# Macaron decoder step: the first two weight chunks multiplied half by half, idle products on TensorE ahead of them, and a pinned order at the start

## The chip, the cores and the metric

The kernel runs on one core of a Trainium2 chip. The metric is the device time of one execution in microseconds (us). TensorE (PE) multiplies, VectorE (DVE), ScalarE (ACT) and GpSimd (POOL) do the elementwise work, and SyncE (SP) issues nearly all DMAs.

## What is computed

Two layers of a decoder trunk, for a prompt of 256 tokens and 8 single-token samples that share all weights. The change touches only what comes first: the input norm and the first SwiGLU block.

```python
def trunk(x, ...):
    for i in range(DEPTH):                      # DEPTH = 2, D_MODEL = 1024, D_FF = 2816
        h = rmsnorm(x, norm_ffn1[i])
        x = x + 0.5 * swiglu(h, w_ffn1_gate[i], w_ffn1_up[i], w_ffn1_down[i])
...
def swiglu(x, w_gate, w_up, w_down):
    return (jax.nn.silu(x @ w_gate) * (x @ w_up)) @ w_down
```

All inputs are float32.

## The kernel before

**Tiling.** The 264 columns (256 prompt tokens, 8 samples) are the moving operand of every projection, with the 1024 features in eight blocks of 128 rows (index k). Weights come in *chunks* of 256 output columns; a chunk has two *halves* of four k blocks, each 128x1024 elements (512 KB). Chunk 0 is gate, chunk 1 is up, and so on in turns. Two output blocks of 128 (index j) make a chunk, each in its own PSUM bank (`pj`).

**Precision.** A product is made of three: the value is split into a rounded part (`xh`, `wh`) and a rest (`xl`, `wl`), and PE adds xh·wh, xl·wh and xh·wl. So each half goes through three steps in class `Weights`: `_load` (L88) issues the DMA to `raw`, `_round` (L98) casts `raw` to `wh`, `_split` (L109) subtracts to get `wl`. There are six `raw` buffers and five each of `wh` and `wl`; a buffer is loaded anew when the step that reads it last is done. `advance` (L125), called from `Flow.tick`, does one split and one round and loads what fits. `W.hi` and `W.lo` say which engine rounds ("s" ACT, "v" DVE) and which splits ("p" POOL, "v" DVE).

**The start.** `start` (L449) loads the samples with the first gains (`small`) and x. PE transposes the samples and gains into `pr` (L474), and the two halves of x, 16 blocks of 128x128, into four PSUM banks `px` (L494). Blocks k and k+4 share a bank. For each k ACT writes `xh` (L322) and DVE `xl` (L324) in `Norm.split`; then DVE copies `px` to `xT` (L503). ACT also sums squares (L485) for the norm; `rsqrt` (L280) and `newton` (L293 to L296) turn them into `rr`, PE spreads `rr` over the partitions (`pb`, L514), and DVE copies that to `R` (L517). The norm factor is applied after the matmul, in `evac`, so the first products need `xh`, `xl` and weights but not `R`.

**The first projection.** `project` with `late_lo` (L360) does chunks 0 and 1 together, 96 matmuls: first all products with `wh` (chunk 0: eight k with xh, eight with xl; then chunk 1), then all with `wl`. Halves are loaded and rounded in the order chunk 0 first half, chunk 0 second half, chunk 1 first half, chunk 1 second half. The first and second are rounded by DVE, the rest by ACT; the first three are split by POOL. From chunk 2 on (L300 to L302), each chunk's three products follow one another for every k.

**Order.** A scheduler places instructions by priority, except those wrapped in `pin` (`tc.keep_in_program_order`), which keep the order in which they are written. Each engine then runs its list strictly in order.

Of the kernel before, what the change touches and what calls it, by code (L numbers as in the profile page):

```python
# [12 lines left out]
ALU = mybir.AluOpType  # L13
# [3 lines left out]
P = 128  # L17
D = 1024
KT = D // P
T = 256  # L20
# [35 lines left out]
class Weights:  # L56
# [31 lines left out]
    def _load(self):  # L88
        i = self.n_load
        parts, n = self.halves[i]  # L90
        raw = self.pool.tile([P, HK, 256], F32, tag="raw", name=f"raw{i}", bufs=RAW_BUFS)
        for src, at in parts:
            dst = raw[:, :n] if len(parts) == 1 else raw.rearrange("p (k s) n -> p k s n", s=2)[:, :, at]
            self.nc.sync.dma_start(dst, src.rearrange("(k p) n -> p k n", p=P))
        self.raw[i] = raw
        self.n_load += 1

    def _round(self):  # L98
# [6 lines left out]
        self.pin(copy(wh[:, :n], self.raw[i][:, :n]))  # L105
        self.ready[i] = wh
        self.n_round += 1

# [108 lines left out]
def trunk_step(ctx: ExitStack, tc: tile.TileContext, ins, consts, outs, stop=None):  # L217
# [69 lines left out]
        act(dst, dst, AF.Exp, scale=-0.5)  # L287

    def newton(dst, src, tmp, scale=1.0, out=None):
        if scale == 1.0:  # L290
            nc.vector.scalar_tensor_tensor(tmp, src, EPS, dst, op0=ALU.add, op1=ALU.mult)
        else:
            nc.vector.tensor_scalar(tmp, src, scale, EPS, op0=ALU.mult, op1=ALU.add)  # L293
            nc.vector.tensor_mul(tmp, tmp, dst)
        nc.vector.scalar_tensor_tensor(tmp, tmp, -0.5, dst, op0=ALU.mult, op1=ALU.mult)
        nc.vector.scalar_tensor_tensor(dst if out is None else out, tmp, 1.5, dst, op0=ALU.add, op1=ALU.mult)  # L296

    def mm3(ps, w, rh, rl, first, last, s=slice(None)):
        wh, wl = w
# [53 lines left out]
    def project(nch, rh, rl, evac, kt_major=2, need=None, before=None, late_lo=False):  # L353
        if not callable(rh):
            rh, rl = (lambda k, t=rh: t[:, k]), (lambda k, t=rl: t[:, k])
        done = 0
        if kt_major:
            ws = [W.get() for _ in range(kt_major)]
            pss = [(c, j, mm_bank(f"pj{c}_{j}")) for c in range(kt_major) for j in range(2)]
            if late_lo:  # L360
                for first in (True, False):
                    for c in range(kt_major):
                        for r in (rh, rl) if first else (rh,):
                            for k in range(KT):
                                w = ws[c](k)[0 if first else 1]
                                for j in range(2):
                                    nc.tensor.matmul(
                                        pss[2 * c + j][2][:, :NC],
                                        w[:, j * P : j * P + P],
                                        r(k),  # L370
                                        start=first and k == 0 and r is rh,
                                        stop=not first and k == KT - 1,
                                    )
                                if k % 4 == 3 and (first or k < KT - 1 or c < kt_major - 1):
                                    flow.tick()
# [37 lines left out]
    def cols(w, c, k0=0, k1=None):  # L413
        return w[k0 : (k1 or w.shape[0]), c * 256 : (c + 1) * 256]

    def add_project(cs, early=False):
        n = 0 if early else 2
        if n:
            W.add(*cs[:n])
        for c in cs[n:]:  # L420
            W.add(c)

    def reg_ffn(name, l):
        cs = [cols(ins[f"w_{name}_{kind}"][l], p) for p in range(FB // 2) for kind in ("gate", "up")]
        add_project(cs, early=name == "ffn1" and l == 0)
# [23 lines left out]
    def start(norm):  # L449
# [13 lines left out]
        nc.vector.memset(ones_d, 1.0 / D)  # L463
        nc.vector.memset(ones_1, 1.0)
        use_set(LNEXP)
        W.preload(4)
        W.pin = pin = tc.keep_in_program_order
        W.lo, W.hi = ("p",), ("v",)
        xn, sm = ring.tiles["x"], ring.tiles["small"]
        with tc.high_priority(offset=1000):  # L470
            ns = NB + 2
            pr = aux_bank("pr")
            for k in range(KT):
                nc.tensor.transpose(pr[:, ns * k : ns * (k + 1)], sm[:ns, k * P : k * P + P], ident[:ns, :ns])  # L474
            prv = pr[:, : ns * KT].rearrange("p (k r) -> p k r", r=ns)
            pin(nc.vector.tensor_copy(gains[:, :, :2], prv[:, :, NB:]))
            xs, gs = prv[:, :, :NB], cp.tile([P, KT, NB], F32, name="gs")
            pin(nc.vector.tensor_copy(xT[:, :, T:], xs))
            pin(nc.vector.tensor_mul(gs, xs, gains[:, :, :1].broadcast_to([P, KT, NB])))
            ss, rr, rt = (cp.tile([P, 3], F32, name=n) for n in ("ss0", "rr0", "rt0"))  # L480
            nc.vector.memset(ss, 1.0)
            junk = memT.rearrange("p k n -> p (k n)")

            def square(i, n, src):
                pin(nc.scalar.activation(junk[:n, :D], src, AF.Square, accum_out=ss[:n, i : i + 1]))  # L485

            square(0, P, xn[:, :D])
            pin(nc.scalar.copy(xh[:, :, T:], gs))
            pin(nc.vector.tensor_sub(xl[:, :, T:], gs, xh[:, :, T:].bitcast(F32)))
            px = [aux_bank("px") if k < 3 else mm_bank("px") for k in range(KT // 2)]  # L490
            px = [b[:, i * T : i * T + T] for i in range(2) for b in px]
            for i in range(2):
                for k in range(KT):
                    nc.tensor.transpose(px[k][:, i * P : i * P + P], xn[:, i * D + k * P : i * D + k * P + P], ident)  # L494
            W.advance()
            for k in range(KT):
                if k == 2:
                    W.advance()
                norm.split(k, px[k], T)
            W.hi = ("s",)  # L500
            W.advance()
            for k in (3, 7, 0, 4, 1, 5, 2, 6):
                pin(nc.vector.tensor_copy(xT[:, k, :T], px[k]))  # L503
            square(1, P, xn[:, D:])
            W.advance()
            square(2, NB, sm[:NB, :D])
            rsqrt(rr, ss, 1.0 / D)
            newton(rr, ss, rt, 1.0 / D)
        W.pin = lambda ins: ins
        W.lo = ("v",)  # L510
        with tc.high_priority(offset=1000):
# [5 lines left out]
            nc.vector.tensor_copy(norm.R, pb[:, :NC])  # L517
        norm.done = True
        use_set(SILU)
        flow.spawn(0, prepare())  # L520

# [978 lines left out]
```

## Time and profile before

| | us |
|---|---|
| median of 3 runs | 1332.32 |
| lowest, highest | 1332.09, 1333.97 |
| the profiled execution, its own time | 1333.74 |
| its span, first to last instruction | 1331.9 |
| PE busy | 1300.5 (98%) |
| DVE, ACT, POOL busy | 842.7, 671.4, 311.2 |

The profiled execution is one run, 1.4 us above the median; times worked out from the trace are compared with its own 1333.74 us. [...]

### The profile page before, as it was taken

The numbers are of one execution on the slowest core, as the hardware profiler recorded it, in microseconds if no ns is written. First come the engines' busy times: TensorE is split into PE (matmuls) and PEld (weight loads), VectorE is DVE, ScalarE is ACT, GpSimd is POOL, SyncE is SP. The second block draws the span as 40 slices with busy tenths as digits, with TensorE's granted clock in tenths as the row PEclk, the third lists the DMA queues.
The fourth block names the chain that finished last, engine by engine and source line by source line (L and its number), as shares of the span: only waits on it lengthen the run. The fifth ranks groups of instructions, "written<-read, shape, count | busy, mean of one in ns | idle before, by whom it ended". The sixth has DMA issues, their size and how long they took to land. (4 is left out here: it accounts for less than half of the span.)

```text
span 1331.9 us, 26153 instructions
## 1 busy us (share of the span) xinstructions
PE 1300.5 (98%) x10420; PEld 1260.0 (95%) x10420; DVE 842.7 (63%) x1586; ACT 671.4 (50%) x1058; POOL 311.2 (23%) x246
## 2 busy tenths in 40 slices
PE   8999999999999999999999999999999997999997
PEld 8999999999879999999999999999998787999996
DVE  6555567769826655465555446968699439766454
ACT  6454444455545555544545545574664445445532
POOL 3211331222641111231111231000015427111220
PEclk9999999999999999999999999999999999999999
DMA  8796565646997666556666566545359994776550
GB/s 278 224 296 186 160 191 182 187 142 220 338 340 230 185 178 186 173 179 188 189 177 182 165 182 187 175 147 174 120 168 300 357 282 127 224 224 204 173 158 34
DMA packets 277435, 266.76 MB, mean 200 GB/s; under 512 B 8697, under 2 KB 275961, under 8 KB 277314
## 3 DMA queue, kind: packets, MB, share of 16 engines
q1 hardware_dynamic: 271486, 259.78, 63.6%
q10 hardware_dynamic: 5828, 5.32, 1.2%
q8 instruction: 82, 1.34, 0.4%
q14 instruction: 39, 0.32, 0.1%
HBM read 255.00 MB, written 10.07 MB: 199 GB/s over the span
## 5 line engine op out<-in xcount | busy, mean ns | idle before, releaser
L117 DVE TENSOR_TENSOR wl<-raw,wh 128x1024 fp32r<-128x1024 f32 (+1 forms) x347 | 431.7, 1249 | 250.3 <-ACT wh L105 235.5
L300 PE MATMUL pj<-xh,wh 128*128 128x264 f32 x1952 | 562.0, 288 | 7.6 <-DVE g L669 5.6
L301 PE MATMUL pj<-xl,wh 128*128 128x264 f32 x1952 | 554.6, 284 | 0.0
L302 PE MATMUL pj<-xh,wl 128*128 128x264 f32 x1952 | 554.0, 284 | 0.0
L105 ACT CAST wh<-raw 128x1024 fp32r<-128x1024 f32 (+1 forms) x406 | 415.0, 1032 | 251.5 <-PE pj L301 132.9
L300 PEld LDWEIGHTS pj<-xh,wh 128*128 128x128 f32 x1952 | 368.8, 189 | 9.9 <-DVE g L669 5.8
L301 PEld LDWEIGHTS pj<-xl,wh 128*128 128x128 f32 x1952 | 369.1, 189 | 0.3
L302 PEld LDWEIGHTS pj<-xh,wl 128*128 128x128 f32 x1952 | 367.4, 188 | 0.0
L300 PE MATMUL dn<-ah,wh 128*128 128x264 f32 x704 | 200.9, 285 | 0.0
L302 PE MATMUL dn<-ah,wl 128*128 128x264 f32 x704 | 200.0, 284 | 0.0
L301 PE MATMUL dn<-al,wh 128*128 128x264 f32 x704 | 199.4, 283 | 0.0
L117 POOL TENSOR_TENSOR wl<-raw,wh 128x1024 fp32r<-128x1024 f32 (+1 forms) x61 | 143.4, 2357 | 205.7 <-ACT wh L105 162.4
L677 POOL TENSOR_TENSOR al<-a,ah 128x264 fp32r<-128x264 f32 x88 | 89.4, 1018 | 412.0 <-ACT ah L676 411.9
L302 PEld LDWEIGHTS dn<-ah,wl 128*128 128x128 f32 x704 | 132.6, 188 | 0.0
L300 PEld LDWEIGHTS dn<-ah,wh 128*128 128x128 f32 x704 | 132.4, 188 | 0.1
L301 PEld LDWEIGHTS dn<-al,wh 128*128 128x128 f32 x704 | 132.5, 188 | 0.0
L280 ACT ACTIVATE g<-g 128x264 f32<-128x264 f32 x88 | 37.0, 424 | 86.5 <-DVE g L669 86.1
L676 ACT CAST ah<-a 128x264 fp32r<-128x264 f32 x88 | 36.1, 413 | 80.3 <-DVE a L675 80.1
L322 ACT ACTIVATE xh<-xT,gains 128x264 fp32r<-128x264 f32 x56 | 28.8, 514 | 77.3 <-DVE xT L703 59.2
L878 DVE CUSTOM_DVE_ANT_0 junk<-ring,pb 128x256 f32<-128x256 f32 x128 | 53.7, 419 | 6.2
L675 DVE TENSOR_TENSOR a<-g,pj 128x264 f32<-128x264 f32 x88 | 37.2, 426 | 30.3 <-PE pj L302 30.3
L669 DVE TENSOR_TENSOR g<-pj,R_norm_ffn 128x264 f32<-128x264 f32 x88 | 37.5, 429 | 29.1 <-PE pj L302 29.0
(323 smaller groups left out, 1543.6 us busy)
## 6 DMA issues: line engine op xcount, KB each, us to landing
raw<-in_w_ffn_gate_dram SPq DMA_DIRECT2D x88, 512.0 KB, 5.8
raw<-in_w_ffn_up_dram SPq DMA_DIRECT2D x88, 512.0 KB, 4.4
raw<-in_w_ffn_down_dram SPq DMA_DIRECT2D x64, 512.0 KB, 3.7
ring<-in_cache_mem_k_dram SPq DMA_DIRECT2D x16, 1024.0 KB, 8.0
raw<-in_w_xkv_dram SPq DMA_DIRECT2D x64, 256.0 KB, 3.7
ring<-in_cache_mem_v_dram SPq DMA_DIRECT2D x16, 1024.0 KB, 11.4
raw<-in_w_rec_in_dram SPq DMA_DIRECT2D x32, 512.0 KB, 4.7
raw<-in_w_ffn_down_dram SPq DMA_DIRECT2D x32, 384.0 KB, 3.1
```

What stands on the lines that cost most here:

```text
L105: self.pin(copy(wh[:, :n], self.raw[i][:, :n]))
L117: self.pin(eng.tensor_sub(wl[:, :n], self.raw.pop(i)[:, :n], wh[:, :n].bitcast(F32)))
L280: in_line(nc.scalar.activation(dst, src, func, **kw))
L300: nc.tensor.matmul(ps, wh[:, s], rh, start=first, stop=False)
L301: nc.tensor.matmul(ps, wh[:, s], rl, start=False, stop=False)
L302: nc.tensor.matmul(ps, wl[:, s], rh, start=False, stop=last)
L322: pin(nc.scalar.activation(h, src, AF.Copy, scale=g))
L669: nc.vector.tensor_mul(g, ps, norm.R)
L675: nc.vector.tensor_mul(a, g, ps)
L676: nc.scalar.copy(ah[:, blk], a)
L677: nc.gpsimd.tensor_sub(al[:, blk], a, ah[:, blk].bitcast(F32))
L878: nc.vector.tensor_tensor_reduce(junk, t[:, b % 4, nt], pb[:, i * XD : i * XD + XD], 1.0, 0.0, ALU.mult, ALU.add, sc[:, nt, h * NB + b : h ...
```

## The change

1. **Half by half.** The halves are now ordered chunk 0 first, chunk 1 first, chunk 0 second, chunk 1 second (`add_project` registers the first two chunks together everywhere). In `project`, the products run over both first halves (xh·wh and xl·wh of chunk 0, then of chunk 1, then xh·wl of each) and then over both second halves in the same way.
2. **Idle products.** Four 128x128 float32 matmuls of `ones_d` with itself ahead of the transposes of the samples, three behind them, into a bank that nobody reads. A float32 matmul is two PE instructions, as the two of each 128-column product of `pb` were.
3. **First weights in two pieces.** The first half is loaded by two DMAs of 256 KB and rounded in two casts of 512 columns, with `xl` of block 0 between them. Six halves are preloaded in place of four.
4. **Who does what, in a fixed order.** DVE rounds the first four halves and POOL splits them; ACT rounds from the fifth. ACT sums the samples' squares first. All of the start, the first projection's matmuls, `newton` and the first splits are pinned. `R` is made in `spread`, which the flow runs among the matmuls of the second halves.

```diff
@@ _load, _round
+            src = src.rearrange("(k p) n -> p k n", p=P)
+            step = HK // 2 if i == 0 else src.shape[1]
+            for a in range(0, src.shape[1], step):
+                self.nc.sync.dma_start(dst[:, a : a + step], src[:, a : a + step])
...
+            self.pin(copy(wh[:, : n // 2], self.raw[i][:, : n // 2]))
+            between()
+            self.pin(copy(wh[:, n // 2 : n], self.raw[i][:, n // 2 : n]))
@@ project
-                for first in (True, False):
-                    for c in range(kt_major):
-                        for r in (rh, rl) if first else (rh,):
-                            for k in range(KT):
+                turns = [(c, hf, lo, r) for hf in range(2) for lo in (0, 1) for c in range(kt_major) for r in ((rh, rl), (rh,))[lo]]
+                for n, (c, hf, lo, r) in enumerate(turns):
+                    for k in range(HK * hf, HK * hf + HK):
...
+                    if n < len(turns) // 2:
+                        flow.tick()
+                    elif n < len(turns) - 1:
+                        flow.step()
+                    if n == len(turns) - 4:
+                        W._round()
...
                     evac(c, j, ps[:, :NC])
+                    if late_lo and c == 0 and j == 1:
+                        W._split()
+                        W.pin = lambda ins: ins
@@ start
+            warm(4)
             for k in range(KT):
-                nc.tensor.transpose(pr[:, ns * k : ns * (k + 1)], sm[:ns, k * P : k * P + P], ident[:ns, :ns])
+                pin(nc.tensor.transpose(pr[:, ns * k : ns * (k + 1)], sm[:ns, k * P : k * P + P], ident[:ns, :ns]))
+            warm(3)
...
+            W._round(between=lambda: splits(0))
+            W._split()
+            splits(1, 2, 3)
+            W._round()
+            W._split()
+            splits(4, 5)
+            W._round()
+            W._split()
+            splits(6, 7)
+            W._round()
+            square(1, P, xn[:, D:])
+            rsqrt(rr, ss, 1.0 / D)
+            for k in (0, 4, 1, 5):
+                pin(nc.vector.tensor_copy(xT[:, k, :T], px[k]))
             newton(rr, ss, rt, 1.0 / D)
+            for k in (2, 6, 3, 7):
+                pin(nc.vector.tensor_copy(xT[:, k, :T], px[k]))
+            W._split()
```

Three places in the instruction lists, before and then after. The line numbers of the changed kernel differ: its L493 is the idle product, L376 the first projection's matmul, L109, L111 and L113 the casts, L333 `xl`, L125 the splits, L302 to L305 `newton`, L541 and L544 the copies to `xT`, L553 `pb`. Numbers behind a name tell buffers apart.

DVE at the start, from the first cast of weights, before (`wh_150` and `wh_162` are the two halves of chunk 0):

```order
L105 CAST wh_150<-raw_102 128x1024
L324 SCALAR_TENSOR_TENSOR xl<-px,gains,xh 128x256 x2
L105 CAST wh_162<-raw_104 128x1024
L324 SCALAR_TENSOR_TENSOR xl<-px,gains,xh 128x256 x6
L503 COPY xT<-px 128x256 x8
L293 TENSOR_SCALAR rt_125<-ss_123 128x3
L117 TENSOR_TENSOR wl_219<-raw_108,wh_195 128x1024
L117 TENSOR_TENSOR wl_245<-raw_152,wh_233 128x1024
L294 TENSOR_TENSOR rt_125<-rt_125,rr_124 128x3
```

And after (`wh_164`, `wh_177`, `wh_185`, `wh_193`: first half of chunk 0, of chunk 1, second half of chunk 0, of chunk 1):

```order
L111 CAST wh_164<-raw_102 128x512
L333 SCALAR_TENSOR_TENSOR xl<-px,gains,xh 128x256
L113 CAST wh_164<-raw_102 128x512
L333 SCALAR_TENSOR_TENSOR xl<-px,gains,xh 128x256 x3
L109 CAST wh_177<-raw_105 128x1024
L333 SCALAR_TENSOR_TENSOR xl<-px,gains,xh 128x256 x2
L109 CAST wh_185<-raw_107 128x1024
L333 SCALAR_TENSOR_TENSOR xl<-px,gains,xh 128x256 x2
L109 CAST wh_193<-raw_109 128x1024
L541 COPY xT<-px 128x256 x4
L302 TENSOR_SCALAR rt_138<-ss_136 128x3
L303 TENSOR_TENSOR rt_138<-rt_138,rr_137 128x3
```

DVE now has four rounds in place of two, and two splits that it did between the steps of `newton` have left that place. `newton` stands behind all four casts.

POOL at the start, before and then after:

```order
masks.py:199 AFFINE_SELECT ident<-ident 128x128
L117 TENSOR_TENSOR wl_160<-raw_102,wh_150 128x1024
L117 TENSOR_TENSOR wl_178<-raw_104,wh_162 128x1024
L117 TENSOR_TENSOR wl_193<-raw_106,wh_180 128x1024
L677 TENSOR_TENSOR al<-a,ah 128x264 x4
```

```order
masks.py:199 AFFINE_SELECT ident<-ident 128x128
L125 TENSOR_TENSOR wl_169<-raw_102,wh_164 128x1024
L125 TENSOR_TENSOR wl_179<-raw_105,wh_177 128x1024
L125 TENSOR_TENSOR wl_187<-raw_107,wh_185 128x1024
L125 TENSOR_TENSOR wl_210<-raw_109,wh_193 128x1024
L718 TENSOR_TENSOR al<-a,ah 128x264 x4
```

POOL has a fourth split, and every one of the four now reads a `wh` that DVE makes.

PE around the spreading of `rr`, before (in the middle of the products with `wl` of chunk 0) and then after (between the two products with `wh_193`, the second half of chunk 1):

```order
L367 MATMUL pj_0_221<-xh,wl_160 128x264
L367 MATMUL pj_1_222<-xh,wl_160 128x264
L367 MATMUL pj_0_221<-xh,wl_178 128x264
L514 MATMUL pb<-ident,rr_124 128x128 x2
L514 MATMUL pb<-ident,rr_124 128x8
L367 MATMUL pj_1_222<-xh,wl_178 128x264
```

```order
L376 MATMUL pj_0_222<-xh,wh_193 128x264
L376 MATMUL pj_1_223<-xh,wh_193 128x264
L553 MATMUL pb<-ident,rr_137 128x128 x2
L553 MATMUL pb<-ident,rr_137 128x8
L376 MATMUL pj_0_222<-xl,wh_193 128x264
L376 MATMUL pj_1_223<-xl,wh_193 128x264
```

Before, 73 matmuls of the first projection stood ahead of `pb` and 23 behind it; after, 72 and 24. Behind the first projection the lists of PE, DVE, ACT, POOL and SP hold the same instructions in the same order as before, apart from one or two rows next to the seam.

## Rows read from the trace of the kernel before

**Rows 1.** The page, busy time and share of the span of each engine, with the number of instructions.

```profile
PE 1300.5 (98%) x10420; PEld 1260.0 (95%) x10420; DVE 842.7 (63%) x1586; ACT 671.4 (50%) x1058; POOL 311.2 (23%) x246
```

**Rows 2.** The timeline of PE, from the start to the first matmul of chunk 2: start, duration of the merged group, engine, line, operation, number of instructions, and in brackets the idle time ahead with what ended it.

```profile
2.75 0.99 PE L474 MATMUL pr<-ident,ring 10*128 10x10 f32 x8 [2.75 <-DMA ring<-in_x_sample_dram]
4.80 3.68 PE L494 MATMUL px<-ident,ring 128*128 128x128 f32 x16 [1.06 <-DMA ring<-in_x_prompt_dram]
8.45 1.56 PE L367 MATMUL pj<-xh,wh 128*128 128x264 f32 x8
11.46 2.01 PE L367 MATMUL pj<-xh,wh 128*128 128x264 f32 x8 [1.45 <-DVE wh L105]
13.26 3.32 PE L367 MATMUL pj<-xl,wh 128*128 128x264 f32 x16
16.42 2.12 PE L367 MATMUL pj<-xh,wh 128*128 128x264 f32 x16
18.37 2.12 PE L367 MATMUL pj<-xl,wh 128*128 128x264 f32 x16
...
21.43 0.92 PE L514 MATMUL pb<-ident,rr 128*128 128x128 f32 x6
22.28 3.04 PE L367 MATMUL pj<-xh,wl 128*128 128x264 f32 x23
25.20 0.36 PE L300 MATMUL pj<-xh,wh 128*128 128x264 f32 x1
```

**Rows 3.** Stretches of one microsecond: length, busy time of PE, PEld, DVE, ACT and POOL (with instructions begun), granted clock, DMA share, GB/s.

```profile
9.00:10.00 1.00, 1.00 (x8) 0.79 (x6) 1.00 (x2) 1.00 (x4) 1.00 (x1) 1.00 1.10 346
10.00:11.00 1.00, 0.01 (x1) 0.00 (x0) 1.00 (x1) 0.17 (x1) 0.76 (x1) 1.00 1.10 348
...
13.00:14.00 1.00, 1.00 (x6) 1.00 (x6) 1.00 (x4) 1.00 (x2) 1.00 (x2) 0.50 1.10 348
...
16.00:17.00 1.00, 1.00 (x10) 1.00 (x10) 0.71 (x3) 1.00 (x3) 0.11 (x1) 1.00 1.10 347
```

**Rows 4.** The timeline of DVE from the first cast of weights to the copy of `R`, columns as in rows 2.

```profile
7.61 0.69 DVE L105 CAST wh<-raw 128x1024 fp32r<-128x1024 f32 x1 [1.22 <-DMA raw<-in_w_ffn_gate_dram]
8.38 0.88 DVE L324 SCALAR_TENSOR_TENSOR xl<-px,gains,xh 128x256 fp32r<-128x256 f32 x2
9.17 2.13 DVE L105 CAST wh<-raw 128x1024 fp32r<-128x1024 f32 x1
11.23 2.43 DVE L324 SCALAR_TENSOR_TENSOR xl<-px,gains,xh 128x256 fp32r<-128x256 f32 x6
13.58 2.73 DVE L503 COPY xT<-px 128x256 f32<-128x256 f32 x8
...
18.95 0.16 DVE L294 TENSOR_TENSOR rt<-rt,rr 128x3 f32<-128x3 f32 x1
...
19.34 0.16 DVE L296 SCALAR_TENSOR_TENSOR rr<-rt,rr 128x3 f32<-128x3 f32 x1
21.57 1.23 DVE L117 TENSOR_TENSOR wl<-raw,wh 128x1024 fp32r<-128x1024 f32 x1 [2.07 <-PE pj L367]
22.71 0.43 DVE L517 COPY R_norm_ffn<-pb 128x264 f32<-128x264 f32 x1
```

**Rows 5.** The timeline of POOL in the same stretch.

```profile
8.39 2.37 POOL L117 TENSOR_TENSOR wl<-raw,wh 128x1024 fp32r<-128x1024 f32 x1 [7.08 <-DVE wh L105]
11.39 4.72 POOL L117 TENSOR_TENSOR wl<-raw,wh 128x1024 fp32r<-128x1024 f32 x2 [0.63 <-DVE wh L105]
```

**Rows 6.** The timeline of DVE at two later places: a split, and an addition to `xT`.

```profile
156.85 2.43 DVE L117 TENSOR_TENSOR wl<-raw,wh 128x1024 fp32r<-128x1024 f32 x1 [3.91 <-ACT wh L105]
...
163.05 2.35 DVE L703 TENSOR_TENSOR xT<-xT,t 128x264 f32<-128x264 f32 x1
```

**Rows 7.** The timeline of POOL at the same two places.

```profile
155.81 2.39 POOL L117 TENSOR_TENSOR wl<-raw,wh 128x1024 fp32r<-128x1024 f32 x1 [6.78 <-PE dn L302]
...
162.71 2.40 POOL L117 TENSOR_TENSOR wl<-raw,wh 128x1024 fp32r<-128x1024 f32 x1 [4.51 <-ACT wh L105]
```

**Rows 8.** All additions of line 703: number, duration in ns (shortest, median, longest), first and last start.

```profile
L703 DVE TENSOR_TENSOR xT<-xT,t x32: 417/433/2351, 159.7 to 1322.3; 128x264 f32<-128x264 f32 x32
```

**Rows 9.** The timeline of ACT at the start.

```profile
7.87 2.30 ACT L322 ACTIVATE xh<-px,gains 128x256 fp32r<-128x256 f32 x6 [1.75 <-PE px L494]
11.74 0.87 ACT L322 ACTIVATE xh<-px,gains 128x256 fp32r<-128x256 f32 x2 [1.56 <-DVE xl L324]
```

**Rows 10.** Two kinds of float32 transposes of 128x128 blocks, all of a line: number, duration in ns (shortest, median, longest), first and last start. `px` is the start, `pm` comes later.

```profile
L494 PE MATMUL px<-ident,ring x16: 421/421/476, 4.8 to 8.1; 128*128 128x128 f32 x16
L555 PE MATMUL pm<-ident,ring x16: 270/271/273, 46.1 to 64.7; 128*128 128x128 f32 x16
```

**Rows 11.** The timeline of PE at one pair of the later transposes.

```profile
54.52 0.38 PE L555 MATMUL pm<-ident,ring 128*128 128x128 f32 x2
```

**Rows 12.** Later stretches, columns as in rows 3: one with a stall of PE in it, and two behind PE's longest stall.

```profile
1036.00:1041.00 5.00, 3.98 (x26) 3.18 (x25) 3.59 (x18) 2.44 (x7) 2.92 (x2) 1.00 1.10 348
...
1128.00:1130.00 2.00, 0.59 (x2) 0.59 (x3) 2.00 (x4) 0.61 (x2) 2.00 (x2) 0.67 0.70 195
1130.00:1135.00 5.00, 5.00 (x24) 5.00 (x24) 3.90 (x8) 1.84 (x4) 2.31 (x3) 0.50 0.41 126
```

**Rows 13.** What PE waited for longest in the whole trace: who for whom, us in total, times, longest us.

```profile
PE pj L300 <- DVE g L669: 5.6, 1, 5.6
```

More of the change, by code (lines that the diff above doesn't have):

```diff
@@ L360, in project @@
             if late_lo:
-                for first in (True, False):
-                    for c in range(kt_major):
-                        for r in (rh, rl) if first else (rh,):
-                            for k in range(KT):
[L365 to L375, printed above, removed]
+                turns = [(c, hf, lo, r) for hf in range(2) for lo in (0, 1) for c in range(kt_major) for r in ((rh, rl), (rh,))[lo]]
+                for n, (c, hf, lo, r) in enumerate(turns):
+                    for k in range(HK * hf, HK * hf + HK):
+                        w = ws[c](k)[lo]
+                        for j in range(2):
+                            tc.keep_in_program_order(
+                                nc.tensor.matmul(
+                                    pss[2 * c + j][2][:, :NC],
+                                    w[:, j * P : j * P + P],
+                                    r(k),
+                                    start=k == 0 and not lo and r is rh,
+                                    stop=k == KT - 1 and lo == 1,
+                                )
+                            )
+                    if n == len(turns) // 2 - 1:
+                        W.release_first_halves(kt_major)
+                    if n < len(turns) // 2:
[4 more added lines that the diff above has]
+                        W._round()
             else:
@@ L414, in cols, with add_project @@
         return w[k0 : (k1 or w.shape[0]), c * 256 : (c + 1) * 256]
[L416 to L420, printed above, removed]
+    def add_project(cs):
+        W.add(*cs[:2])
+        for c in cs[2:]:
             W.add(c)
@@ L424, in reg_ffn @@
         cs = [cols(ins[f"w_{name}_{kind}"][l], p) for p in range(FB // 2) for kind in ("gate", "up")]
-        add_project(cs, early=name == "ffn1" and l == 0)
+        add_project(cs)
         for o in range(4):
@@ L465, in start @@
         use_set(LNEXP)
-        W.preload(4)
+        W.preload(6)
         W.pin = pin = tc.keep_in_program_order
@@ L471, in start, with warm @@
             ns = NB + 2
-            pr = aux_bank("pr")
+            def warm(n):
+                for _ in range(n):
+                    pin(nc.tensor.matmul(idle[:, :P], ones_d, ones_d, start=True, stop=True))
+            pr, idle = mm_bank("pr"), mm_bank("idle")
+            warm(4)
             for k in range(KT):
-                nc.tensor.transpose(pr[:, ns * k : ns * (k + 1)], sm[:ns, k * P : k * P + P], ident[:ns, :ns])
+                pin(nc.tensor.transpose(pr[:, ns * k : ns * (k + 1)], sm[:ns, k * P : k * P + P], ident[:ns, :ns]))
+            warm(3)
             prv = pr[:, : ns * KT].rearrange("p (k r) -> p k r", r=ns)
@@ L485, in square @@
                 pin(nc.scalar.activation(junk[:n, :D], src, AF.Square, accum_out=ss[:n, i : i + 1]))
-            square(0, P, xn[:, :D])
+            square(2, NB, sm[:NB, :D])
             pin(nc.scalar.copy(xh[:, :, T:], gs))
             pin(nc.vector.tensor_sub(xl[:, :, T:], gs, xh[:, :, T:].bitcast(F32)))
-            px = [aux_bank("px") if k < 3 else mm_bank("px") for k in range(KT // 2)]
+            square(0, P, xn[:, :D])
+            px = [aux_bank("px") for _ in range(KT // 2)]
             px = [b[:, i * T : i * T + T] for i in range(2) for b in px]
@@ L493, in start, with splits, spread @@
                 for k in range(KT):
[L494 to L502, printed above, removed]
+                    pin(
+                        nc.tensor.transpose(px[k][:, i * P : i * P + P], xn[:, i * D + k * P : i * D + k * P + P], ident)
+                    )
+            def splits(*ks):
+                for k in ks:
+                    norm.split(k, px[k], T)
+            W._round(between=lambda: splits(0))
[11 more added lines that the diff above has]
+            for k in (0, 4, 1, 5):
                 pin(nc.vector.tensor_copy(xT[:, k, :T], px[k]))
[L504 to L507, printed above, removed]
             newton(rr, ss, rt, 1.0 / D)
-        W.pin = lambda ins: ins
-        W.lo = ("v",)
-        with tc.high_priority(offset=1000):
+            for k in (2, 6, 3, 7):
+                pin(nc.vector.tensor_copy(xT[:, k, :T], px[k]))
+            W._split()
+            W.lo, W.hi = ("v",), ("s",)
+        def spread():
+            for _ in range(8):
+                yield
             pb = aux_bank("pb")
@@ L516, in start @@
                 )
-            nc.vector.tensor_copy(norm.R, pb[:, :NC])
-        norm.done = True
+            pin(nc.vector.tensor_copy(norm.R, pb[:, :NC]))
+            norm.done = True
+        flow.spawn(2, spread())
         use_set(SILU)
```

18 lines of the change are left out of this document (10 added, 8 removed).

## The prediction

> **What bounds the kernel now.** I read the page first: PE is busy for 98% of the span [rows 1], so only PE's time counts, and a start that is shortened moves all the rest forward. Then PE's timeline at the start [rows 2]. The 96 matmuls of the first projection run from 8.45 to 25.20, 16.75 us. At full rate one takes 0.122 us (16 from 16.42 to 18.37), so 96 take 11.7, and `pb` 0.85 (21.43 to 22.28). So 4.2 us are lost there, and that is what the change can win inside the projection; ahead of it lies what could be won by starting earlier than 8.45. [...] First a wait of 1.45 us for the second cast of DVE [rows 2]. [...] And the first matmuls are fed one block at a time by ACT. From 25.20 on PE waits seldom; its longest wait is one of 5.6 us [rows 13], far behind.
>
> **Why the wait is there** decides this case. DVE's first cast took 0.69 us, the second, of the same shape, 2.13: it began at 9.17 and ended at 11.30 [rows 4], while POOL's split ran from 8.39 to 10.76 [rows 5]. So the cast did its work in the 0.54 us behind POOL's end. Its data were there when it began. Later rows show the same: a split on DVE that begins 1.04 us behind one on POOL takes 2.43 in place of 1.23, and an addition of two SBUF operands takes 2.35 in place of 0.43, each ending just behind POOL's [rows 6 to 8, 4]. `xl` (one operand in PSUM) and the copies to `xT` (from PSUM) kept their pace of 0.39 and 0.33 beside POOL's second and third split [rows 4, 5].
>
> **The change, part by part.**
>
> *Idle products* run where PE waited for x (1.06 us idle ahead of 4.80, more ahead of 2.75) [rows 2], so they cost nothing but a start of the transposes at about 5.1: 8 instructions, the samples' transposes (1.0), 6 instructions, each 0.22 at the low clock, from about 1.1 on. They buy clock. The 16 transposes of x took 3.68 us, 421 ns each and 0.217 apart; the same operation later takes 271 ns, and the two of a pair take 0.38 together, so 0.11 apart [rows 2, 10, 11]. [...] ACT's first `xh` came at 7.87 [rows 9], when the 13th transpose was done (4.80 + 12 x 0.217 + 0.42 = 7.82): block 0 waits for its bank mate, block 4 of x's second half. x's second half lands between the first (4.80) and the first weights (7.61) [rows 2, 4]; three transfers of equal size in one queue, so about 6.2, an estimate. With the clock up: 6.2 + 4 x 0.11 + 0.27 = 6.9, and `xh` of block 0 is ready at 7.4 in place of 8.35. That is the first gain, 0.9 us.
>
> *Two pieces, and half by half.* The first 256 KB land at about 6.9, so the first piece is cast in time. DVE then does `xl` of block 0 (7.45 to 7.85) and the second piece's cast to 8.22. PE's demand is now: chunk 0's first half (16 matmuls), then chunk 1's first half, whose cast is DVE's second whole one. The change reorders the demand but leaves the pair that collided: POOL's split of the first half begins at 8.3 and DVE's cast of the next half is queued behind three `xl` (to 9.5).
>
> *Four rounds on DVE against four splits on POOL* is the term that sets the sum. Each cast stands beside a running split, and each split needs the cast before it. One turn is 0.09 (cast to split) + 2.37 (split) + 0.54 (cast behind it) = 3.00 us [rows 4, 5]. From 8.22: casts end at 11.2, 14.2 and 17.2; splits end at 10.7, 13.7, 16.7 and 19.7. Loads don't matter, since they come every 1.5 us (512 KB at 348 GB/s) [rows 3]: 9.1, 10.6, 12.1.
>
> *`newton` behind the casts.* DVE does four copies to `xT` (1.4 us, to 18.6) and then `newton`, whose second step reads two SBUF operands, while the fourth split runs to 19.7. Queued behind it are three small steps and then `pb` on PE, which waits for `rr`, and behind `pb` 24 matmuls. The three steps took 0.55 (18.95 to 19.50) [rows 4], so `rr` at 20.2. No row shows a 128x3 operation beside POOL. The nearest, of 128x264, was held to the end [rows 6 to 8], and I take that; the other bound is that small ones pass, `rr` at 19.3. [...]
>
> *PE's side.* It starts at 7.45, is fed by ACT and by `xl` and is through chunk 0's first half at 9.8; waits to 11.25 (1.45 us, the same wait as before); 32 matmuls to 15.15, 16 more to 17.1, a wait of 0.15, 8 more to 18.2; then 2.0 us for `rr`. The wait before is not removed, and a second one stands where PE had none.
>
> *Sum.* `rr` 20.2 + `pb` 0.85 + 24 x 0.122 = 24.0 for the first matmul of chunk 2, against 25.20: 1.2 us gained. The pins and the two further DMA issues on SP cost nothing: those queues wait for transfers anyhow (DMA share 1.10) [rows 3]. Behind the seam, DVE has to make the splits of chunk 2: four copies to 21.6, a split (1.23) to 22.9, `R` (0.43), two `g` of that shape, and a split to 25.3, wanted at 24.0 + 12 x 0.122 = 25.5. That cover is 0.2 us thin; late by as much, it costs as much. From there on the lists are the same. The sum is against the profiled execution: 1333.74 - 1.2 = 1332.5. The median, 1332.32, lies 1.4 below that execution; part of this may be the low clock of the start, which another execution need not meet, so against the median the gain may be nothing.
>
> **The rivals.** What a measurement of this kernel can tell from no change is about 0.2%, 2.7 us.
>
> 1. *The casts are not held, PE alone is the bound.* Then casts end by 13 and splits by 18; PE goes on from 9.8 with 80 matmuls (9.8) and `pb` (0.85) and a few tenths of waits: 20.7, a gain of 4.5, 1329.2. Against it stands the pair in rows 4 and 5.
> 2. *Small steps pass POOL.* 0.9 less: 1331.6.
> 3. *The clock falls once more in the wait for `rr`.* It fell behind a wait of 1.45 with thin work around it [rows 2, 3]; a stretch with PE busy for 3.98 of 5.00 us kept 1.00 [rows 12]. The new wait of 2.0 is longer but has denser work around. About 3.8 us of work follow; 3.4 us at the low clock cost some 1.6 (0.22 in place of 0.122 for 16 matmuls): 1334.1. A fall behind the first wait would be free, since DVE and POOL set the end then.
> 4. *Slower: the clock falls there and stays down for long.* After PE's longest wait (5.6 us [rows 13]) it stood at 0.50 through 1130 to 1135 and for part of 1128 to 1130 [rows 12]. If the low clock covers `pb`, the 24 matmuls and three more microseconds of chunk 2, it costs 6.8 x 0.45 = 3.1: 27.1, 1.9 behind before, 1335.6. [...]
> 5. *The idle products don't lift the clock in time.* Transposes from 5.1 at 0.217: block 4 of the second half ends at 5.1 + 12 x 0.217 + 0.42 = 8.1, 1.2 later than in the sum; the whole chain moves: 1333.7. [...]
>
> **How the numbers follow.** The forecast (1332.5) 0.52, rival 1 0.06, rival 2 0.12, rival 3 0.16, rival 4 0.05, rival 5 0.09. Faster by over 0.2% is rival 1 alone: 0.06, and 0.01 for a sum that is better than all: 0.07. Slower by over 0.2% is rival 4: 0.05. The rest, 0.88, is within 0.2%. The range holds the forecast and rivals 2, 3 and 5 with half a microsecond to spare, the spread seen in before's runs taken in: 1331.0 to 1334.5; rivals 1 and 4 stay out.
>
> **What would show it.** Right: DVE's second, third and fourth whole cast take 1.7 to 2.2 us in place of 0.69 and end 0.5 behind POOL's splits; PE waits 1.4 us for a cast and 2 us for `rr` ahead of `pb`; transposes of x at 271 ns; the first matmul of chunk 2 at about 24. Wrong: casts of 0.7 us beside running splits, `rr` before 19, a granted clock of 0.50 behind 18, or chunk 2 waiting for its own splits.

## The result and the profile after

| | before | after |
|---|---|---|
| median, us | 1332.64 (20 runs) | 1335.03 (20 runs) |
| lowest, highest | 1331.49, 1333.97 | 1332.91, 1337.39 |
| profiled execution, its span | 1333.74, 1331.9 | 1332.91, 1331.1 |
| PE busy | 1300.5 | 1300.2 |

The ratio of after to before is 1.0019, with a 95% interval of 1.0012 to 1.0026: slower, by about the least that can be told from no change. The forecast was 1332.5 with a range of 1331.0 to 1334.5, so the median fell out of it at the upper end. Two things stand out before any row is read. The profiled execution of the changed kernel was the fastest of its 20. And the times lie in three groups, not around one value. Further executions of the same kernel (the first and the last three runs below, the last three on a second chip) fill the same groups; of 35 in all, 14 lie at 1332.91 to 1334.08, 12 at 1334.99 to 1336.00 and 9 at 1336.80 to 1337.54.

The start of the profiled execution goes as predicted in its mechanism. PE's timeline, against [rows 2] (columns as there):

```profile
5.52 2.60 PE L521 MATMUL px<-ident,ring 128*128 128x128 f32 x16
8.35 1.67 PE L376 MATMUL pj<-xh,wh 128*128 128x264 f32 x8 [0.24 <-ACT xh L331]
...
12.31 1.21 PE L376 MATMUL pj<-xh,wh 128*128 128x264 f32 x8 [1.31 <-DVE wh L109]
...
18.28 1.22 PE L376 MATMUL pj<-xh,wh 128*128 128x264 f32 x8
21.50 0.99 PE L553 MATMUL pb<-ident,rr 128*128 128x128 f32 x6 [2.00 <-DVE rr L305]
...
25.45 0.28 PE L309 MATMUL pj<-xh,wh 128*128 128x264 f32 x1
```

Two waits, 1.31 us for a cast and 2.00 for `rr`, and chunk 2 at 25.45; before it began at 25.20 [rows 2]. DVE's timeline, against [rows 4]:

```profile
8.33 0.49 DVE L333 SCALAR_TENSOR_TENSOR xl<-px,gains,xh 128x256 fp32r<-128x256 f32 x1 [0.94 <-ACT xh L331]
8.73 0.42 DVE L113 CAST wh<-raw 128x512 fp32r<-128x512 f32 x1
...
10.24 1.92 DVE L109 CAST wh<-raw 128x1024 fp32r<-128x1024 f32 x1
...
12.87 2.32 DVE L109 CAST wh<-raw 128x1024 fp32r<-128x1024 f32 x1
...
15.90 2.33 DVE L109 CAST wh<-raw 128x1024 fp32r<-128x1024 f32 x1
...
19.48 1.22 DVE L302 TENSOR_SCALAR rt<-ss 128x3 f32<-128x3 f32 x1
20.80 0.16 DVE L303 TENSOR_TENSOR rt<-rt,rr 128x3 f32<-128x3 f32 x1
...
21.19 0.16 DVE L305 SCALAR_TENSOR_TENSOR rr<-rt,rr 128x3 f32<-128x3 f32 x1
```

And POOL's, against [rows 5]:

```profile
9.23 2.38 POOL L125 TENSOR_TENSOR wl<-raw,wh 128x1024 fp32r<-128x1024 f32 x1 [7.93 <-DVE wh L113]
12.24 2.39 POOL L125 TENSOR_TENSOR wl<-raw,wh 128x1024 fp32r<-128x1024 f32 x1 [0.63 <-DVE wh L109]
...
18.30 2.36 POOL L125 TENSOR_TENSOR wl<-raw,wh 128x1024 fp32r<-128x1024 f32 x1 [0.63 <-DVE wh L109]
```

The second cast piece, done at 9.15, releases the first split. Each of the three whole casts ends about 0.55 us behind a split (12.16 behind 11.61, for one), and a turn is 3.02 us. The first step of `newton` is held too: 1.22 us, to the end of the fourth split. What this trace does not show is why the kernel is usually slower than in it. PE's clock does not fall in its start. Stretches of 1 us, columns as in [rows 3]; the granted clock is a share of PE's full speed, and it is 1.00 in every stretch from 19 to 26:

```profile
20.00:21.00 1.00, 0.00 (x0) 0.00 (x0) 0.86 (x3) 0.35 (x1) 0.66 (x1) 1.00 0.87 299
...
23.00:24.00 1.00, 1.00 (x11) 1.00 (x10) 1.00 (x2) 0.26 (x1) 0.00 (x0) 1.00 1.08 398
```

### The profile page after: what moved, and what is told of

It reads as the page before. It is cut to its first block, busy times and chain, and to the rows that moved or that the text cites. A ratio compares the mean times of both kernels' runs of the same rounds, so it can differ in the third digit from the quotient of the medians.

```text
span 1331.1 us, 26190 instructions
## 1 busy us (share of the span) xinstructions
PE 1300.2 (98%) x10434; PEld 1259.3 (95%) x10434; DVE 847.2 (64%) x1588; ACT 670.2 (50%) x1056; POOL 314.9 (24%) x247
## 3 DMA queue, kind: packets, MB, share of 16 engines
q8 instruction: 82, 1.34, 0.4%
## 5 line engine op out<-in xcount | busy, mean ns | idle before, releaser
L125 DVE TENSOR_TENSOR wl<-raw,wh 128x1024 fp32r<-128x1024 f32 (+1 forms) x346 | 430.5, 1249 | 246.0 <-ACT wh L109 235.9
L109 ACT CAST wh<-raw 128x1024 fp32r<-128x1024 f32 (+1 forms) x404 | 413.3, 1032 | 259.5 <-PE pj L310 134.5
L125 POOL TENSOR_TENSOR wl<-raw,wh 128x1024 fp32r<-128x1024 f32 (+1 forms) x62 | 145.9, 2358 | 207.8 <-ACT wh L109 169.6
L342 POOL TENSOR_TENSOR nacc_norm_xattn<-nacc_norm_xattn,nsq 128x264 f32<-128x264 f32 x14 | 12.8, 915 | 183.0 <-ACT nsq L341 182.7
```

The costliest lines, as they stand in the source:

```text
L125: self.pin(eng.tensor_sub(wl[:, :n], self.raw.pop(i)[:, :n], wh[:, :n].bitcast(F32)))
```

## The experiments

The theory: in most executions the clock falls in the wait for `rr`, and this, with a later rise of the clock ahead of the transposes of x, is what lies between the profiled execution and the median. Its rivals: something behind the start, or the held casts by themselves. Of the runs that follow, those that were timed have 11 or 12 executions; ratios are to the kernel before on the same chip. A trace is one profiled execution; the first trace of the changed kernel is the one shown above.

**The changed kernel again**, unedited.

> The changed kernel once more, unedited, for a second trace. Theory (the clock falls in the 2.0 us in which PE waits for rr, in a part of the executions, and a fall costs about 1.6 us for a short low stretch and 3.2 us for a long one): the runs spread over some 4 us, 1333 to 1337, and a trace of a run above 1334.5 shows a granted clock of 0.50 behind 20 us; one below shows 1.00 there. Rival (the spread comes from elsewhere, from the 5.6 us stall late in the program or from the time at which the clock rises ahead of the transposes): a trace above 1334.5 shows 1.00 from 18 us to the late stall.

Median 1335.28, ratio 1.0016 [1.0007, 1.0024]; the profiled execution took 1335.18 and so belongs to the middle group. PE's timeline and stretches of 1 us of this second trace:

```profile
5.51 3.62 PE L521 MATMUL px<-ident,ring 128*128 128x128 f32 x16
...
22.23 1.06 PE L553 MATMUL pb<-ident,rr 128*128 128x128 f32 x6 [2.00 <-DVE rr L305]
23.22 2.13 PE L376 MATMUL pj<-xl,wh 128*128 128x264 f32 x8
...
27.67 0.28 PE L309 MATMUL pj<-xh,wh 128*128 128x264 f32 x1
```

```profile
22.00:23.00 1.00, 0.77 (x6) 0.68 (x6) 1.00 (x5) 0.00 (x0) 0.00 (x0) 1.00 0.36 56
23.00:24.00 1.00, 1.00 (x5) 0.98 (x6) 1.00 (x3) 0.00 (x0) 0.00 (x0) 0.51 0.95 317
...
26.00:27.00 1.00, 1.00 (x9) 1.00 (x8) 0.22 (x1) 0.47 (x1) 0.00 (x0) 0.78 0.92 372
```

The wait is the same 2.00 us, but behind it the granted clock reads 0.51 and 0.50 until past 26: eight matmuls take 2.13 us in place of 1.24. Chunk 2 comes 2.22 us later than in the first trace. Of that, 0.73 was there when `pb` began (22.23 against 21.50): the transposes took 3.62 us in place of 2.60, nearly the 3.68 of before [rows 2]; in the first trace one of them takes 421 ns at most and 273 in the median. That they ran at the low clock is read from this pace: the granted clock is listed as 1.00 from 5 to 6 us in both traces. The other 1.49 is the fall.

**Idle products in the wait**: the changed kernel, with eight idle products ahead of `pb`, in PE's wait for `rr`.

```diff
             pb = aux_bank("pb")
+            for _ in range(8):
+                pin(nc.tensor.matmul(pb[:, 3 * P :], ones_d, ones_d, start=True, stop=True))
```

> [...] Theory (the clock falls in that wait): the slow executions vanish, all runs lie at 1332.8 to 1334.3, median about 1333.5. Rival (the spread comes from elsewhere): spread and median stay, 1333 to 1337 about 1335.

Median 1333.28 (1332.83 to 1334.91), ratio 1.0005 [0.9997, 1.0014]. PE's timeline:

```profile
19.37 1.95 PE L553 MATMUL pb<-ones_d 128*128 128x128 f32 x16
21.43 1.02 PE L555 MATMUL pb<-ident,rr 128*128 128x128 f32 x6
...
25.41 0.28 PE L309 MATMUL pj<-xh,wh 128*128 128x264 f32 x1
```

`rr` comes no earlier and nothing else moved, yet of 11 executions none is above 1334.91, where 21 of 35 were. Filling PE's idle time takes the two slower groups away, so it was PE's standing still that made them. The times show this, not the trace: its transposes took 2.61 us, and no trace of the changed kernel with transposes as short has a fall.

**`newton` ahead of the fourth cast.**

```diff
+            square(1, P, xn[:, D:])
+            rsqrt(rr, ss, 1.0 / D)
+            newton(rr, ss, rt, 1.0 / D)
             W._round()
-            square(1, P, xn[:, D:])
-            rsqrt(rr, ss, 1.0 / D)
-            for k in (0, 4, 1, 5):
-                pin(nc.vector.tensor_copy(xT[:, k, :T], px[k]))
-            newton(rr, ss, rt, 1.0 / D)
-            for k in (2, 6, 3, 7):
+            for k in (0, 4, 1, 5, 2, 6, 3, 7):
```

> newton stands ahead of DVE's fourth cast, and the eight copies to xT behind it. Theory (newton was held by POOL's fourth split, and PE's wait for rr makes the clock fall): newton now waits for POOL's third split, rr is there at about 18.3, the fourth cast takes 0.7 us with no split beside it, PE waits 0.7 us for it and not for rr, and chunk 2 begins at 23.8 in place of 25.45: median about 1331.9, spread under 2 us. Rival (the spread comes from elsewhere): the 1.6 us are won, but the spread stays at 4 us, median about 1333.4.

Median 1332.89 (1331.65 to 1333.53), ratio 0.9999 [0.9990, 1.0007]. DVE's timeline and then PE's:

```profile
16.28 1.81 DVE L302 TENSOR_SCALAR rt<-ss 128x3 f32<-128x3 f32 x1
...
18.67 0.69 DVE L109 CAST wh<-raw 128x1024 fp32r<-128x1024 f32 x1
```

```profile
19.41 1.24 PE L376 MATMUL pj<-xh,wh 128*128 128x264 f32 x8 [0.63 <-DVE wh L109]
20.49 0.92 PE L551 MATMUL pb<-ident,rr 128*128 128x128 f32 x6
```

The hold is moved to where it hurts less: the third split (15.65 to 18.06) holds `newton`'s first step for 1.81 us, and the cast behind it, with no split running, takes 0.69. The wait of 2.00 is now one of 0.63, and the slower groups are gone. The median of 1331.9 that was expected was missed by 1.0: chunk 2 begins at 24.36, 0.84 earlier than in the first trace of before, and still the median is no better than before's.

**Three casts on ACT**: the second to the fourth half are rounded by ACT.

```diff
             W._split()
+            W.hi = ("s",)
             splits(1, 2, 3)
```

> ACT rounds the second to fourth half in place of DVE, between its xh; POOL still splits. Theory (DVE's casts are held by POOL's splits): the casts take 1.05 us each on ACT beside running splits, the second half is rounded by 10.4 in place of 12.2, the wait of 1.3 us for it is gone, POOL's splits follow one another without a gap and end at 18.8, rr is there at about 19.4, chunk 2 begins at about 23: median about 1331. Rival (the casts are late because of their loads or of the xl ahead of them): PE's wait for the second half stays at over 1 us.

Median 1332.05 (1331.33 to 1332.99), ratio 0.9993 [0.9985, 1.0002]. ACT's timeline and then DVE's:

```profile
9.97 1.06 ACT L109 CAST wh<-raw 128x1024 fp32r<-128x1024 f32 x1
...
13.29 1.10 ACT L109 CAST wh<-raw 128x1024 fp32r<-128x1024 f32 x1
```

```profile
15.47 1.61 DVE L302 TENSOR_SCALAR rt<-ss 128x3 f32<-128x3 f32 x1 [0.15 <-ACT memT L510]
17.20 2.24 DVE L303 TENSOR_TENSOR rt<-rt,rr 128x3 f32<-128x3 f32 x1
```

On ACT a cast beside a running split takes 1.06 to 1.10 us, and the wait for the second cast is gone. POOL, never waiting for a cast now, runs its four splits in a row (9.94 to 19.42) and holds two steps of `newton`, each to the end of a split. `rr` is waited for only 1.04 us, and chunk 2 begins at 23.93 (about 23 was expected).

**Without the idle products**: the changed kernel less `warm(4)` and `warm(3)`.

```diff
-            warm(4)
...
-            warm(3)
```

> The changed kernel without its idle products; all else as it is. Theory (the products buy no clock in most executions, and they push the first transpose of x from 4.80 to 5.51): the transposes of x start at 4.8 again, ACT's first xh at 7.9, 0.6 earlier than in the second look at the changed kernel, the two waits of 1.3 and 2.0 us stay, and so does the fall in the second one in part of the executions: 1334.7, still slower than before. Rival (the idle products lift the clock early, and without them the low clock reaches further into the first projection): 1336 or more.

Median 1334.38 (1332.88 to 1336.64), ratio 1.0014 [1.0005, 1.0023]. The transposes begin at 4.74 and take 3.67 us, ACT's first `xh` begins at 7.81, the two waits are 0.78 and 2.00 us, and chunk 2 comes at 25.44, as in the first trace of the changed kernel. The products bought nothing there that could be measured. The slower groups stay, but in this trace the clock does not fall in the wait for `rr`: the eight matmuls behind `pb` take 1.24 us.

**The idle products alone**: the kernel before, with four and three idle products as in the change, and the transposes pinned.

```diff
+            warm(4)
             for k in range(KT):
-                nc.tensor.transpose(pr[:, ns * k : ns * (k + 1)], sm[:ns, k * P : k * P + P], ident[:ns, :ns])
+                pin(nc.tensor.transpose(pr[:, ns * k : ns * (k + 1)], sm[:ns, k * P : k * P + P], ident[:ns, :ns]))
+            warm(3)
```

> The kernel before with the idle products alone (four ahead of the samples' transposes, three behind), and the transposes pinned. Theory: the transposes of x start at 5.5 in place of 4.80, and where the clock rises late, at 9 or 10 us, all behind them comes 0.7 later: 1333.4; where it rises at 7, nothing is won or lost: 1332.8. Rival (idle products lift the clock for the transposes, as the forecast had it): xh at 7.4 and 0.5 to 0.9 faster: 1332.0.

Median 1332.15 (1331.10 to 1333.43), ratio 0.9998 [0.9989, 1.0007]. The profiled execution, 1331.10, was the fastest of its own. PE's timeline of it:

```profile
11.58 1.71 PE L367 MATMUL pj<-xh,wh 128*128 128x264 f32 x8 [0.92 <-DVE wh L105]
13.13 2.10 PE L367 MATMUL pj<-xl,wh 128*128 128x264 f32 x16
...
23.86 0.36 PE L300 MATMUL pj<-xh,wh 128*128 128x264 f32 x1
```

Neither the theory's reason nor the rival's holds in this trace. The transposes begin at 5.51 and `xh` only at 8.53, later than before [rows 9]; but POOL's split ends when it did, so the wait for the cast shrinks to 0.92 from 1.45, and here the clock does not fall behind it (granted clock 1.00 from 11 to 16): 16 matmuls take 2.10 us where they took 3.32 [rows 2]. How often that is so was not measured; by the medians the gain is 0.45 us, within the noise.

**The kernel before again**, one trace.

> The kernel before, unedited, a second look. Theory (the clock's falls and rises stand at other places in each execution): the waits and durations of DVE, ACT and POOL are the same as in the first look, and the time lies within its 1331.3 to 1334.4, with the low clock at other places in the first 26 us or after the late wait. Rival (before always has its fall behind the wait of 1.45 us, at the same place): granted clock 0.50 from 11.5 to 15.5 again, and chunk 2 at 25.2 within 0.2.

1332.37. The clock falls behind the wait for the second cast again (1.43 us; 0.50 from 13 to 16), and chunk 2 begins at 25.52, even later than in the first trace. The 1.37 us between the two traces lie elsewhere, behind PE's longest wait [rows 12, 13]: over 1115 to 1145 the granted clock is 0.89 in the first and 0.94 in this. PE takes up its work there at 1129.41 and 1129.54, and the low clock ends at 1135.5 and at 1132.4, so 3.2 us less of the work ran at it. In the first trace a matmul behind that wait starts every 0.220 us at a granted clock of 0.50 and every 0.121 at 1.00, so 0.45 of each such microsecond is lost, the prediction's price: some 1.4 us, an estimate.

**ACT's casts and an early `newton`**: as with three casts on ACT, and the last sum of squares, `rsqrt` and `newton` moved ahead of POOL's first split; the load of the next activation table is pinned behind the casts.

```diff
+            square(1, P, xn[:, D:])
+            rsqrt(rr, ss, 1.0 / D)
-            W._round(between=lambda: splits(0))
+            def between():
+                newton(rr, ss, rt, 1.0 / D)
+                splits(0)
+            W._round(between=between)
             W._split()
+            W.hi = ("s",)
...
             W._round()
-            square(1, P, xn[:, D:])
-            rsqrt(rr, ss, 1.0 / D)
-            for k in (0, 4, 1, 5):
-                pin(nc.vector.tensor_copy(xT[:, k, :T], px[k]))
-            newton(rr, ss, rt, 1.0 / D)
-            for k in (2, 6, 3, 7):
+            table = nc.scalar.preload_act_table_set(SILU)
+            pin(table)
+            in_line(table)
+            loaded[0] = SILU
+            for k in (0, 4, 1, 5, 2, 6, 3, 7):
```

> The changed kernel with the second, third and fourth cast of weights on ACT, and with newton ahead of POOL's first split: ACT sums x's second half right when it has landed, and DVE does the four small steps behind the first cast piece. Theory (what the changed start loses is DVE steps held beside POOL's splits, and the clock that falls in the waits which they make): no step of the first projection is held any longer, PE has no wait for a cast and none for rr, the clock stays up, and 96 matmuls at 0.122 us, pb (0.85) and a few tenths of feeding behind the first at 9.06 (the place in the run with ACT's casts) put chunk 2 at 22.0, 1.9 earlier than there: 1330.1. Rival (the bound moves to chunk 2's own splits, which DVE cannot begin before POOL's fourth split ends, at about 19.5): chunk 2 begins at 22 but waits, and the time stays at 1332.

Median 1331.18 (1329.72 to 1331.77), ratio 0.9988 [0.9979, 0.9996]. DVE's timeline and then PE's:

```profile
7.50 0.16 DVE L302 TENSOR_SCALAR rt<-ss 128x3 f32<-128x3 f32 x1
7.94 0.16 DVE L303 TENSOR_TENSOR rt<-rt,rr 128x3 f32<-128x3 f32 x1 [0.28 <-ACT rr L288]
```

```profile
9.05 1.77 PE L376 MATMUL pj<-xh,wh 128*128 128x264 f32 x8
...
18.76 0.92 PE L560 MATMUL pb<-ident,rr 128*128 128x128 f32 x6
...
22.63 0.28 PE L309 MATMUL pj<-xh,wh 128*128 128x264 f32 x1
```

PE has no wait between the first matmul and chunk 2, `newton`'s steps take 0.16 us, and chunk 2 begins 1.30 us earlier than with ACT's casts alone. The median moved 0.87, to 1331.18 where 1330.1 was expected. Part of the reason is seen at PE's longest wait. Its timeline there, in the first trace of the changed kernel and then in this one:

```profile
1129.92 0.59 PE L309 MATMUL pj<-xh,wh 128*128 128x264 f32 x1 [5.62 <-DVE g L710]
```

```profile
1127.09 0.59 PE L309 MATMUL pj<-xh,wh 128*128 128x264 f32 x1 [5.62 <-DVE g L717]
```

PE takes up its work 2.83 us earlier, but the low clock behind the wait ends at nearly the same time, 1133.3 and 1133.2 (granted clock 0.84 and 0.90 over 1133 to 1134). So 6.1 us of work run at the low clock in place of 3.4, which costs some 1.2 us at the same price. (It was 5.5 in the trace with `newton` ahead of the fourth cast, which missed its time too.) Chunk 2 is 2.82 earlier between these traces, and the span only 1.4 shorter.

Here and in the two other kernels with ACT's casts, 2.05 to 2.09 us of the profiled execution lie outside the span, against 1.74 to 1.87 in the rest; where that quarter of a microsecond goes was not found.

**The same without the idle products.**

> The kernel with ACT's casts and the early newton (chunk 2 at 22.63, 1331.18), without the idle products. Theory (where PE has no wait that lets the clock fall, the idle products only hold back the transposes of x, 5.51 in place of 4.74): all of the start comes 0.7 earlier, chunk 2 at 21.9 to 22.2, 1330.6. [...]

Median 1331.01 (1330.44 to 1332.01), ratio 0.9984 [0.9975, 0.9993], on the second chip, where the median of before is 1333.36: the best of all, though not told apart from the run above. The expected 0.7 us did not come; chunk 2 begins at 22.71. ACT's timeline suggests why:

```profile
6.89 1.06 ACT L508 ACTIVATE memT<-ring 128x1024 f32<-128x1024 f32 x1 [0.80 <-DMA ring<-in_x_prompt_dram]
...
8.51 1.55 ACT L331 ACTIVATE xh<-px,gains 128x256 fp32r<-128x256 f32 x4
```

In this execution x's second half landed 0.7 us later than in the run above (6.89 against 6.19), and the sum of squares and `rsqrt`, which now stand ahead of `xh` on ACT, ended just when `xh` began.

**Three more traces of the changed kernel**, to see what the third group is.

> The changed kernel, unedited, a third look, since 13 of its 32 times lie at 1332.9 to 1334.1, 12 at 1335.0 to 1336.0 and 7 at 1336.8 to 1337.4. Theory: the first kind has no fall of the clock in the start, the second has one of 3.4 us in or behind the wait for rr, the third has one of twice that length or two of them, and all have the same waits of 1.3 and 2.0 us. Rival: the kinds differ behind the start (in or behind the late wait of 5.6 us) and all have the start of one of the first two looks.

> The changed kernel, unedited, a fourth look; as of the third: by the theory its time is told by the number and length of the stretches with a granted clock of 0.50 before 30 us (none: 1333 to 1334; one of 3.4 us: 1335 to 1336; more: 1337), by the rival by what lies behind 1100 us.

> The changed kernel, unedited, a fifth look; as of the third and the fourth: none, one or more stretches with a granted clock of 0.50 before 30 us give 1333 to 1334, 1335 to 1336 or 1337 by the theory; by the rival they say nothing of the time.

The third trace took 1333.34: transposes in 2.72 us, no fall (granted clock 1.00 from 19 to 26), chunk 2 at 25.57. The fourth and fifth took 1337.35 and 1337.54. PE's timeline (to 29 us, one matmul short of chunk 2) and stretches of 1 us of the fourth:

```profile
5.51 3.39 PE L521 MATMUL px<-ident,ring 128*128 128x128 f32 x16
...
22.22 1.72 PE L553 MATMUL pb<-ident,rr 128*128 128x128 f32 x6 [1.99 <-DVE rr L305]
23.87 2.13 PE L376 MATMUL pj<-xl,wh 128*128 128x264 f32 x8
25.79 3.44 PE L376 MATMUL pj<-xh,wl 128*128 128x264 f32 x15
```

```profile
22.00:23.00 1.00, 0.78 (x4) 0.81 (x4) 1.00 (x5) 0.00 (x0) 0.00 (x0) 0.59 0.39 91
...
28.00:29.00 1.00, 1.00 (x6) 1.00 (x6) 1.00 (x3) 0.76 (x2) 0.00 (x0) 0.50 0.53 181
29.00:30.00 1.00, 1.00 (x10) 1.00 (x9) 1.00 (x3) 0.15 (x1) 0.00 (x0) 0.99 0.25 81
```

The wait is 1.99 us once more, and now the clock is down from 22 to 29, over `pb`, all 24 matmuls and on to chunk 2, which begins at 29.19: 3.74 us later than in the first trace, 0.72 of it there at `pb` and 3.02 the fall. The fifth trace reads the same (29.21). So the three groups are no fall, a short one and a long one, with one or two traces for each. Behind the start the fourth trace has this:

```profile
1133.56 0.59 PE L309 MATMUL pj<-xh,wh 128*128 128x264 f32 x1 [5.60 <-DVE g L710]
```

PE ends its longest wait 3.64 us later than in the first trace, so nearly all of the delay was there at chunk 2, and the rival that put the difference behind the start is out for the most part. But the times differ by 4.4: behind the wait the low clock lasts to 1138.3, over 4.8 us of work in place of 3.4, some 0.6 us more. The granted clock over 1115 to 1145, 0.89 in all five traces, does not tell this.

## Why the prediction was wrong

**The hold was read rightly.** "Each cast stands beside a running split" held closely: a turn of 3.02 us where 3.00 was summed, casts of 1.92 to 2.33 us, a wait of 1.31 for a cast (1.45 forecast) and of 2.00 for `rr` (2.0 forecast). Rivals 1 and 2 are out. Small steps do not pass POOL: `newton`'s first step, with one SBUF operand, was held for 1.22, 1.81 and 1.61 us in three kernels, and the second for 2.24. The forecast had only the second held. The hold of the first cost 0.2 us: `rr` came 1.15 behind the forecast, where POOL's splits were 0.96 behind it.

**The step that failed is the chance of rivals 3 and 4**, "the clock falls once more in the wait for `rr`" and "stays down for long". They were given 0.16 and 0.05 because the work around the wait is denser than around the wait of before, and because one stretch with PE busy for 3.98 of 5.00 us kept its clock [rows 12]. In 35 executions the fall came, by their times, in 12 and in 9. The prices were right: 1.6 and 3.1 us were worked out for 3.4 and 6.8 us at the low clock (before's start has 0.50 for 3.4 us, from 12.5 to 15.9), and 1.49 and 3.02 were measured, over 3.4 and 6.8. One stretch that kept its clock was read as a rule, when the same wait of 2.00 us with the same work around it lets the clock fall in one execution and not in the next. In the five traces it goes with the start: where the transposes took 2.60 and 2.72 us, so that by their pace the clock rose during them, it did not fall; where they took 3.39, 3.41 and 3.62, so that it rose later, it did. That one makes the other is not shown: without the idle products, a trace with transposes of 3.67 us and the same wait of 2.00 us kept its clock. Both differ between executions of the one kernel: by the transposes, 2.60 to 3.62 us, the rise comes early or late, and the fall came at 23.0, at 22.2 or not at all. The prediction asked this of the rise (rival 5) and should have asked it of the fall as well.

**The gain of 0.9 us ahead of the first product was mis-sized.** The forecast had `xh` of block 0 ready at 7.4. DVE begins its `xl` at 8.33 in the first trace, and ACT begins `xh` at 8.53 in three of the five. The idle products themselves hold the first transpose back to 5.51, which before began at 4.80 [rows 2]; in the best case the faster transposes (2.60 us) pay that back, and in the other (3.39 to 3.62) they do not, and all behind is 0.7 late. That is rival 5, given 0.09, met in three of five traces. Even in the first trace every later term is this 0.9 behind: POOL's fourth split ends at 20.66 and not at 19.7. With the held step of `newton` and 0.3 us between `rr` and chunk 2 (4.1 where 3.8 was summed), chunk 2 begins at 25.45 and not at 24.0. So the gain of 1.2 us in the sum was gone even without a fall: that trace has chunk 2 0.25 later than before's first trace and 0.07 earlier than its second.

**The 1.4 us between profile and median of before** were put partly on the low clock of the start. The second trace of before has that too; the difference lay behind PE's longest wait. So the sum set out from an execution that was 1.0 to 1.1 us longer behind chunk 2 than the first two traces of the changed kernel (1333.74 - 25.20 against 1332.91 - 25.45 and 1335.18 - 27.67). This hides part of the miss: chunk 2 in the second trace is 3.67 behind the sum (1.45 as in the first, 0.73 for the late transposes, 1.49 for the fall), its time 2.7 above the forecast. That the executions without a fall lie in the stated range is luck in part, since two errors of 1.1 and 1.45 us nearly cancel there. Nor does a shorter start simply move all the rest forward, as the prediction had it: the low clock behind the late wait ended at 1133.3 and at 1133.2 in two traces in which PE took up its work 2.83 us apart.

**What stays open.** The 14 executions without a fall have a median of 1333.44, 0.8 above before's 1332.64, while the traces put the two starts within 0.4 us of each other. Behind the late wait the low clock covers 6.1 and 2.9 us of work in the two traces of before, 3.4 and 3.3 in the two of the changed kernel without a fall, so the traces do not show where the 0.8 lies. What decides in an execution whether the clock falls in the wait, and for how long, was not found. A copy of the changed kernel with no split on POOL was not tried.

## What to carry to other kernels

When two engines hold each other, as DVE's casts and POOL's splits do here, don't move more steps to one of them: with four casts on DVE in place of two, PE had two waits, of 1.31 and 2.00 us, where one of 1.45 had been. Give the held steps to an engine that is not held (a cast took 1.06 us on ACT and 2.3 on DVE beside the same split), and put short steps that others wait for ahead of the first long one (a step of `newton` took 0.16 us ahead of the splits and up to 2.24 beside one). A new wait on TensorE is priced at its length and, with the chance that several executions show, at the low clock behind it, which here cost 1.5 or 3.0 us behind a wait of 2.0. One trace tells the mechanism and not the median: look where the profiled execution lies among the times before the sum is made, and where times lie in groups, take a trace of one of each.

## What was not expected of the hardware

The same wait of 2.00 us left the clock at 1.00, or was followed by 0.50 from 23.0 to 26.4, or from 22.2 to 29.0, in executions of one kernel, and the wait of 1.30 to 1.34 us ahead of it was followed by a fall in none of the five (eight matmuls behind it took 1.21 or 1.22 us). In the kernel before, both traces show a fall behind a wait of 1.45 and 1.43 us. A step on 128x3 elements, 0.16 us alone, took up to 2.24 us beside a split. And the low clock behind PE's longest wait ended at 1133.3 and 1133.2 in two traces in which PE took up its work 2.83 us apart.
